# Attention's matmul order drawn by a planner with a charge on each change of kind

## The chip, the cores and the metric

The kernel runs on one core of a Trainium2 chip. The metric is the device time of one execution in microseconds. Three timed runs before the change gave 1975.88, 1974.33 and 1975.59 us, median 1975.59. One more execution was taken with the hardware profiler: its time was 1973.83 us and its span, from the first instruction to the end of the last, 1972.1 us. A difference of about 0.2% (4 us) is what a measurement of this kernel can tell from none.

## The reference

One layer of a hybrid encoder on 1024 positions of width 1024, all in float32. Three token mixers run on the same normalised input; their outputs are gated and summed; a gated feed-forward network follows. Two of the mixers are attention with 8 heads each. Cut to what matters here:

```
def blocked_attention(q, k, v, bias_mask):      # Q_BLOCK = 128, S = 1024
    def one_block(args):
        i, q_blk = args
        s = einsum('bqhd,bkhd->bhqk', q_blk, k) * scale
        p = softmax(bias_mask(i, s), axis=-1)
        return einsum('bhqk,bkhd->bqhd', p, v)

y_a = mla_branch(u_mla, ...) @ w_br_mla          # attention, 8 heads, masked by chunks of 64
y_b = fox_branch(u_fox, ...) @ w_br_fox          # attention, 8 heads, causal, with a decay
y_c = ssm_branch(u_ssm, ...) @ w_br_ssm          # state-space scan in chunks
g = sigmoid(u_gate + b_gate)                     # u_gate = hn @ w_in[..., gate columns]
x = x + (g0 * y_a + g1 * y_b + g2 * y_c) @ w_out
x = x + conv_ffn(rms_norm(x), ...)
```

## The kernel before

Every float32 product is made on TensorE (PE) from a high and a low part of each operand, so most products are three matmuls: high by high, low by high, high by low. The program goes through the layer in stages: projections, the two attentions, the state-space scan, the branch outputs with their gates, the output projection, the feed-forward network. The change lies in the attention stage, from 534.5 to 877 us of the profiled span.

**What the stage does.** There are 16 heads (8 of the first attention, then 8 of the second). Each head has 8 rows of 128 queries; row `i` sees `i + 1` blocks of 128 keys, so its scores are 128 to 1024 columns wide. Two rows make a unit, four units a head. PE does four kinds of work in the stage, named here by the letters of the planner:

- **S**, scores (line 1899, three or two passes a row in pieces of 256 to 512 columns; line 1903 adds the causal mask to the last piece of the second attention's rows). A row's scores stand in a PSUM tile `s`, of which there are two.
- **T**, transposes (line 1966): the normalised probabilities `pm` are turned block by block into a PSUM tile `tp`, up to four blocks to a tile, of which there are two.
- **V**, the product with the values (lines 1978 to 1986): four or five matmuls a tile, added up in PSUM tile `o`.
- **F**, filler (line 1588): the gate columns of the input projection, which nobody in the stage waits for. It comes in steps of six matmuls of 512 columns. What is left of it when the stage ends is done in the state-space scan and shared out there.

Between them stand the other engines. After S, VectorE (DVE) takes the row's maximum (`nmx`, line 1913), ScalarE (ACT) the exponential (`pm`, line 1918), DVE the reciprocal of the sum (`rs`, line 1924), GpSimd (POOL) multiplies by it (line 1926); then T can start. After T, ACT copies the high part (`pth`, line 1970) and DVE subtracts it for the low part (`ptl`, line 1974); then V can start. After the last V of a unit ACT and DVE bring `o` out (lines 1946 and 1950). The scores of a row wait for the exponential of the row two before it, since that frees the tile `s`.

**What sets the order.** PE, ACT, DVE and POOL run in this stage in an order that is fixed when the program is built, and each of them takes its instructions strictly in that order. A planner, class `Sim` from line 1698, draws it: it has a duration and a pace for each task, keeps a clock for each engine, and puts down one instruction after another. For PE it holds one list each for S, T and V and the filler, and `pick_pe` chooses among the heads of the lists that can start earliest; where several can start within 0.02 us, the letters of `ORDER` decide. Filler goes in when nothing else can start within `SLACK`, or when the share of filler done is behind the share of work done (`total` and `lead`).

```
mm_cost(w, n) = n * (w + 32) / 2400        # us for n matmuls of w columns
c = 0.109 * len(offs)                      # us for a tile of transposes
ORDER = "VTS"
sm = Sim(fill, 86, work, 2.0)              # total filler 86 us, lead 2 us
```

Behind the stage, line 2063 shares the filler that is left among the chunks of the scan: `FILL_SSD = [(f_left[0] - 6.0 - 23.0) / 8] * 8 + [12.0, 24.5]`. There `merge` interleaves the pieces of three chunks with filler, for PE alone.

## Time and profile before

| | before |
|---|---|
| median of three runs | 1975.59 us (1974.33 to 1975.88) |
| profiled execution, time | 1973.83 us |
| its span | 1972.1 us |
| granted TensorE clock over the span | 0.999 |
| attention stage, first score to last value product | 534.5 to 876.9 us |
| matmuls in it: S, T, V, F | 544, 576, 704, 444 |
| changes from one kind to another in it | 377 |
| scan behind it, up to the branch products | 877 to 1067 us |

The counts of kinds and changes are those of the program's order; the profile's own rows carry the line numbers by which the kinds are told. A row of the timeline begins with the time at which the instruction started and its duration, both in us. Matmuls overlap: one takes some 0.3 to 0.4 us from start to end, but the next starts 0.06 to 0.23 us after it. So the time that PE needs for a run of matmuls is read from start to start, not from the durations, and PE counts as busy even where it is not at its quickest.

### The profile page before, as it was taken

The page shows a single profiled execution, that of the slowest core. Times are in us where ns is not written, and L with a number is a line of the kernel's source. Part 1 is how long each engine was busy: PE and PEld are TensorE (multiplying, and loading weights), DVE is VectorE, ACT ScalarE, POOL GpSimd, SP SyncE. Part 2 cuts the span into 40 slices and gives each one's busy share as a digit, 9 for nine tenths or more (in the row PEclk, how much of TensorE's full clock was granted, in tenths as well). Part 3 has the DMA queues.
Part 4 walks back from the last instruction along what each step waited for, and adds up shares of the span by engine and source line. Part 5 has one row for each costly group of instructions (what it writes and reads, how often), then busy time and mean ns, then how long its engine had stood idle before and what let it go on. Part 6 is the DMA issues. An engine that isn't in the chain of part 4 may idle for free.

```text
span 1972.1 us, 28446 instructions
## 1 busy us (share of the span) xinstructions
PE 1949.2 (99%) x10053; PEld 1658.6 (84%) x10053; DVE 1401.0 (71%) x2178; ACT 976.9 (50%) x1690; POOL 699.9 (35%) x666
## 2 busy tenths in 40 slices
PE   9999999999999999999999999999999999999999
PEld 8989878888899988887888888888878888888887
DVE  7777769579566676758884575568997877765555
ACT  5555324454566666657783222225544444444432
POOL 5133100166133333213331451102664454423665
PEclk9999999999999999999999999999999999999999
DMA  6166755532757666635646875434222211259575
GB/s 181 53 198 212 202 132 155 187 102 91 227 167 195 177 179 169 170 95 194 214 152 228 291 252 184 139 107 127 94 90 86 76 53 54 86 166 337 185 262 191
DMA packets 281673, 318.46 MB, mean 161 GB/s; under 512 B 19405, under 2 KB 209497, under 8 KB 281530
## 3 DMA queue, kind: packets, MB, share of 16 engines
q1 hardware_dynamic: 281528, 316.64, 51.6%
q8 instruction: 79, 1.29, 0.3%
q14 instruction: 64, 0.52, 0.1%
q10 hardware_dynamic: 2, 0.00, 0.0%
HBM read 223.46 MB, written 93.13 MB: 161 GB/s over the span
## 4 chain that ended last, share of the span: by engine, by line
PE 86%; DVE 5%; issue 3%; ACT 2%; DMA 2%; POOL 1%; SPq 1%; ACTq 0%; DVEq 0%; POOLq 0%
PE dn L2760 10%; PE mm L1588 10%; PE ybr L2328 7%; PE cb L1384 7%; PE ua L2419 6%; PE uc L2419 5%; PE ud L2419 5%; PE wo L2464 4%; PE s L1899 4%; PE fx L798 3%; PE fx L1134 3%; PE tp L1966 3%; PE ub L2419 2%; PE fxv L188 2%; PE py L2172 1%
## 5 line engine op out<-in xcount | busy, mean ns | idle before, releaser
L2760 PE MATMUL dn<-dr,dr 128*128 128x512 f32 x592 | 182.3, 389 | 0.0
L1926 POOL TENSOR_SCALAR pm<-pm,rs 128x128 f32<-128x128 f32 (+7 forms) x128 | 95.3, 747 | 227.1 <-DVE rs L1924 203.6
L1588 PE MATMUL mm<-hnh,wh 128*128 128x512 f32 x320 | 132.6, 414 | 0.3 <-ACT t L1566 0.3
L2760 PEld LDWEIGHTS dn<-dr,dr 128*128 128x128 f32 x592 | 111.2, 188 | 22.9
L1588 PE MATMUL mm<-hnh,wl 128*128 128x512 f32 x320 | 125.7, 393 | 0.0
L1918 ACT ACTIVATE pm<-s,nmx 128x128 f32<-128x128 f32 (+7 forms) x128 | 94.8, 741 | 61.6 <-DVE nmx L1913 52.3
L1588 PE MATMUL mm<-hnl,wh 128*128 128x512 f32 x320 | 125.2, 391 | 0.0
L2760 PE MATMUL dn<-dr 128*128 128x512 f32 x296 | 115.3, 390 | 0.0
L1974 DVE TENSOR_TENSOR ptl<-tp,pth 128x512 fp32r<-128x512 f32 (+1 forms) x160 | 96.8, 632 | 23.7 <-ACT pth L1970 22.4
L135 DVE TENSOR_TENSOR dr<-dr,dr 128x1024 fp32r<-128x1024 f32 x52 | 71.4, 1380 | 51.7 <-ACT dr L134 44.4
L135 DVE TENSOR_TENSOR wl<-S,wh 128x1024 fp32r<-128x1024 f32 x55 | 81.4, 1480 | 35.6 <-ACT wh L134 35.5
L1913 DVE TENSOR_REDUCE nmx<-s 128x1 f32<-128x128 f32 (+7 forms) x128 | 93.4, 748 | 16.0 <-PE s L1899 9.3
L2328 PE MATMUL ybr<-ah,wl 128*128 128x512 f32 x256 | 99.8, 390 | 0.7 <-DVE wl L135 0.7
L2328 PE MATMUL ybr<-al,wh 128*128 128x512 f32 x256 | 99.9, 390 | 0.0
L2328 PE MATMUL ybr<-ah,wh 128*128 128x512 f32 x256 | 99.7, 390 | 0.0
L134 ACT ACTIVATE wh<-wr 128x1024 fp32r<-128x1024 f32 (+1 forms) x47 | 42.4, 902 | 104.6 <-PE ybr L2328 41.2
L1970 ACT ACTIVATE pth<-tp 128x512 fp32r<-128x512 f32 (+1 forms) x160 | 82.7, 553 | 23.1 <-PE tp L1966 21.2
L134 ACT ACTIVATE wh<-S 128x1024 fp32r<-128x1024 f32 x55 | 58.3, 1059 | 67.4 <-PE uc L2419 45.9
L134 ACT ACTIVATE dr<-dr 128x1024 fp32r<-128x1024 f32 x52 | 54.9, 1060 | 71.8 <-PE dn L2760 52.9
L1966 PE MATMUL tp<-ident,pm 128*128 128x128 f32 x576 | 80.9, 273 | 0.2 <-POOL pm L1926 0.2
L135 DVE TENSOR_TENSOR wl<-wr,wh 128x1024 fp32r<-128x1024 f32 (+1 forms) x47 | 54.5, 1159 | 32.9 <-ACT wh L134 32.8
L2637 DVE SCALAR_TENSOR_TENSOR fa<-cg,pc_f,fa 128x1023 f32<-128x1023 f32 (+1 forms) x44 | 74.2, 1688 | 1.4 <-ACT fa L2632 1.4
(665 smaller groups left out, 6219.4 us busy)
## 6 DMA issues: line engine op xcount, KB each, us to landing
dr<-act_d SPq DMA_DIRECT2D x99, 256.0 KB
wr<-in_w_in_dram SPq DMA_DIRECT2D x35, 512.0 KB
raw<-in_w_in_dram SPq DMA_DIRECT2D x27, 512.0 KB
gl<-g_d SPq DMA_DIRECT2D x24, 512.0 KB
wr<-in_ffn_w_up_dram SPq DMA_DIRECT2D x23, 512.0 KB
ws<-in_ffn_w_down_dram SPq DMA_DIRECT2D x22, 512.0 KB
wsum_d<-ws SPq DMA_DIRECT2D x22, 512.0 KB
act_d<-fa SPq DMA_DIRECT2D x22, 512.0 KB
```

Source lines behind the costliest of these rows:

```text
L134: i = A.activation(h, src, AF.Copy) if he is A else he.tensor_copy(h, src)
L135: return i, le.tensor_sub(l, src, f32(h))
L1384: T.matmul(ps, a, b, start=first and i == 0, stop=i == 11, skip_group_check=not first)
L1588: T.matmul(ps, a[:, k, :], b[half][:, k, :], start=(k == 0 and i == 0), stop=(k == NK - 1 and i == 2))
L1913: V.reduce_max(r.nmx[:, 0:1], r.row, axis=AX, negate=True)
L1918: A.activation(r.p[:, 0:cols], r.row, AF.Exp, bias=r.nmx[:, 0:1], accum_out=r.rs[:, 0:1])
L1926: r.norm = Task("G", (d - 0.025, d), lambda: G.tensor_scalar(r.p[:, 0:cols], r.p[:, 0:cols], r.rs[:, 1:2], 0.0, op0=ALU.mult, op1=ALU.add) ...
L1966: T.transpose(x.pt[:, c * P:c * P + P], rows_[qi].p[:, k * P:k * P + P], ident)
L1974: V.tensor_sub(x.tl[:, :off], x.pt[:, :off], f32(x.th[:, :off]))
L2328: T.matmul(pss[half], w_[:, k, :], a_[k][:, hs], start=k == 0 and i == 0, stop=k == nk - 1 and i == 2)
L2419: T.matmul(ps, a, b, start=first and n == 0, stop=n == 11, skip_group_check=not first)
L2760: T.matmul(ps[m], a[:, ts_], b[:, 512:], start=first_ and j == 0 and q == 0, stop=j == NFH - 1 and q == 2, skip_group_check=not first_)
```

## The change

Only the planner's rules change, and so the order in which the same instructions stand. The planner gets a table `SWITCH` with a charge in us for each change from one kind to another (`"TS"`: from transposes to scores), which moves its clock forward, or back where the charge is negative. V must be startable 0.6 us and T 0.4 us longer before they count as ready (`MARGIN`). While it is in a run of S or V it stays there as long as the next of that kind can start (`STICKY`). Once it is in filler, filler counts as behind until it is 2.8 us ahead (`HYST`). Of kinds that are ready together, T now goes first, then V, then S. The total of filler that it aims at in the stage goes from 86 to 80.

```diff
     LATE = 0.09
+    SWITCH = {"TS": 0.155, "TF": 0.117, "TV": 0.122, "SV": 0.088, "SF": 0.075, "FV": 0.037, "VS": 0.035, "VF": 0.051,
+              "VT": -0.049, "ST": -0.039, "FT": -0.075}
+    STICKY, HYST = "SV", 2.8
+    MARGIN = {"V": 0.6, "T": 0.4}
...
-            self.free["P"] = start + c
+            self.free["P"] = start + c + self.enter("F")
...
+        def enter(self, q):
+            x = SWITCH.get(self.kind + q, 0.0)
+            self.kind = q
+            return x
...
-                        c.append((max(x, f), n, st[0], q))
-            t0 = min([e[0] for e in c], default=None)
+                        c[q] = (max(x + MARGIN.get(q, 0.0), f), st[0], q, max(x, f))
+            t0 = min([e[0] for e in c.values()], default=None)
...
-                behind = self.used < self.total * min(1.0, self.worked / self.work) + self.lead
+                due = self.total * min(1.0, self.worked / self.work) + self.lead
+                behind = self.used < due + (HYST if self.kind == "F" else 0.0)
...
-                    e = min((e for e in c if e[0] <= t0 + 0.02), key=lambda e: e[1])
-                    return e[0], e[2], e[3]
+                    if self.kind in STICKY and self.kind in c and c[self.kind][0] <= t0 + 0.03:
+                        return c[self.kind][3], *c[self.kind][1:3]
+                    for q in ORDER:
+                        if q in c and c[q][0] <= t0 + 0.02:
+                            return c[q][3], *c[q][1:3]
...
+                    st += self.enter(q)
                     self.place(x[1], st)
...
-    ORDER = "VTS"
+    ORDER = "TVS"
...
-            sm = Sim(fill, 86, work, 2.0)
+            sm = Sim(fill, 80, work, 2.0)
```

In the stage's order the changes of kind go from 377 to 335, by kind:

| from, to | S-T | S-V | S-F | T-S | T-V | T-F | V-T | V-S | V-F | F-S | F-T | F-V |
|---|---|---|---|---|---|---|---|---|---|---|---|---|
| before | 21 | 42 | 36 | 67 | 14 | 27 | 83 | 14 | 5 | 17 | 4 | 47 |
| now | 45 | 10 | 23 | 18 | 80 | 10 | 27 | 53 | 18 | 6 | 36 | 9 |

Runs of scores become longer (78 runs instead of 99 for the same 544 matmuls), runs of filler fewer (51 for 68), runs of transposes stay 108. Of the filler, 444 matmuls stood in the stage and now 384: 12 go ahead of its first score and 48 behind its last value product. Lines behind the insertions have moved by 4 to 15, so 1899, 1966 and 1978 are 1914, 1981 and 1993 now.

On PE, at a value product in the middle of the first attention, before: the transposes into `tp_6588`, the scores of two rows, and then at once the product that reads the copies of the transposes just made (`pth_6597` is the copy of the tile ahead of `tp_6588`, `pth_6599` that of `tp_6588` itself).

```order
L1966 MATMUL tp_6588<-ident,pm_6450 128x128
L1966 MATMUL tp_6588<-ident,pm_6507 128x128 x2
L1899 MATMUL s_6593<-w0h_6268,w0l_6269 128x512 x3
L1899 MATMUL s_6593<-w0h_6268,w0l_6269 128x384 x3
L1899 MATMUL s_6606<-w0h_6268,w0l_6269 128x512 x3
L1978 MATMUL o<-pth_6597,vv_6274 128x256
...
L1978 MATMUL o<-pth_6599,vv_6274 128x256
```

On PE at the like place now (`pth_7095` is the copy of `tp_7082`):

```order
L1981 MATMUL tp_7082<-ident,pm_6955 128x128
L1981 MATMUL tp_7082<-ident,pm_6969 128x128 x2
L1914 MATMUL s_7089<-w0h_6883,w0l_6884 128x384 x3
L1914 MATMUL s_7089<-w0h_6883,w0l_6884 128x256 x3
L1914 MATMUL s_7104<-w0h_6883,w0l_6884 128x384 x6
L1981 MATMUL tp_7113<-ident,pm_7012 128x128
...
L1981 MATMUL tp_7119<-ident,pm_7077 128x128
...
L1993 MATMUL o<-pth_7069,vv_6578 128x256
...
L1993 MATMUL o<-pth_7095,vv_6578 128x256
```

Both rows' scores now stand in one run, and the next seven transposes have moved in between, so a product stands further behind the transposes that it needs.

On PE, at the scores of a fifth row of the second attention (`s_10053`, 640 columns), before. It takes the place in PSUM of the third row, `s_9994`:

```order
L1899 MATMUL s_9994<-w0h_9803,w0l_9804 128x384 x2
...
L1899 MATMUL s_10000<-w0h_9803,w0l_9804 128x512 x2
...
L1588 MATMUL mm_10011<-hnh_118,wh_9539 128x512
...
L1978 MATMUL o<-pth_9989,vv_9521 128x256
...
L1966 MATMUL tp_10040<-ident,pm_9893 128x128
...
L1966 MATMUL tp_10045<-ident,pm_9905 128x128 x2
L1899 MATMUL s_10053<-w0h_9803,w0l_9804 128x384 x2
```

On PE at the same rows of another head now (`s_9455` takes the place of `s_9408`):

```order
L1914 MATMUL s_9408<-w0h_9206,w0l_9207 128x384 x2
...
L1914 MATMUL s_9415<-w0h_9206,w0l_9207 128x512 x2
...
L1993 MATMUL o<-pth_9395,vv_8875 128x256
...
L1993 MATMUL o<-pth_9401,vv_8875 128x256
...
L1981 MATMUL tp_9435<-ident,pm_9388 128x128 x2
L1914 MATMUL s_9455<-w0h_9206,w0l_9207 128x384 x2
```

Six matmuls of filler, eight of values and seven transposes stood between the fourth row's scores and the fifth's; now nine of values and three transposes do.

On PE at the start of the scan, where `p6`, the six matmuls of line 2146 on `xddh` and `xddl`, wait for their operands; before:

```order
L2117 MATMUL stp_10742<-bc_10622 128x128 x2
L2104 MATMUL stp_10796<-ident,xs_10626 128x128 x4
L1588 MATMUL mm_10722<-hnh_119,wh_10551 128x512
...
L2146 MATMUL pst_10819<-xddh_10754,bTh_10737 128x512
L2146 MATMUL pst_10819<-xddl_10755,bTh_10737 128x512
```

and now:

```order
L2132 MATMUL stp_10682<-bc_10562 128x128 x2
L1588 MATMUL mm_10662<-hnh_119,wh_10475 128x512
...
L2119 MATMUL stp_10750<-ident,xs_10566 128x128 x4
L1588 MATMUL mm_10761<-hnh_118,wh_10625 128x512
...
L2161 MATMUL pst_10777<-xddh_10694,bTh_10677 128x512
L2161 MATMUL pst_10777<-xddl_10695,bTh_10677 128x512
```

A second block of twelve filler matmuls has moved in ahead of the wait. Behind the scan all engines keep their order.

## The prediction

> **What bounds the kernel now.** I read the busy shares and the chain that ended last first, then the stretches by stage, the waits of PE in the stage, and the timeline where PE changes its kind of work.

> ```profile
> PE 1949.2 (99%) x10053; PEld 1658.6 (84%) x10053; DVE 1401.0 (71%) x2178; ACT 976.9 (50%) x1690; POOL 699.9 (35%) x666
> PE 86%; DVE 5%; issue 3%; ACT 2%; DMA 2%; POOL 1%; SPq 1%; ACTq 0%; DVEq 0%; POOLq 0%
> 532.00:877.00 345.00, 342.82 (x2280) 303.95 (x2278) 234.71 (x489) 227.04 (x510) 121.16 (x148) 1.00 0.60 163
> 877.00:900.00 23.00, 20.77 (x96) 16.88 (x97) 10.37 (x11) 14.00 (x34) 5.72 (x2) 0.97 0.94 316
> 900.00:1067.00 167.00, 165.66 (x929) 142.29 (x929) 127.15 (x175) 120.39 (x248) 51.46 (x77) 0.99 0.52 166
> ```

> The stretches give, after their length, the busy time of PE, of its weight loads, of DVE, ACT and POOL, then the granted clock and DMA. PE is busy for 342.8 of the attention stage's 345 us at the full clock, while DVE and ACT have a third of their time free. So the stage lasts as long as PE's own stream of matmuls, and an order can win two things: the time that PE loses in changing from one kind to another, and the short stops in which it waits for ACT, DVE or POOL. How large the first is, the starts tell:

> ```profile
> 540.07 0.29 PE L1978 MATMUL o<-pth,vv 128*128 128x256 f32 x1
> 540.19 0.22 PE L1983 MATMUL o<-pth,vv 128*64 128x128 f32 x1
> 540.25 0.22 PE L1984 MATMUL o<-pth,vv 128*64 128x128 f32 x1
> ...
> 541.43 0.93 PE L1966 MATMUL tp<-ident,pm 128*128 128x128 f32 x7
> 542.12 0.77 PE L1899 MATMUL s<-w0h,w0l 104*128 104x384 f32 x3
> 542.73 0.40 PE L1588 MATMUL mm<-hnh,wh 128*128 128x512 f32 x1
> 542.97 0.39 PE L1588 MATMUL mm<-hnl,wh 128*128 128x512 f32 x1
> 543.19 0.39 PE L1588 MATMUL mm<-hnh,wl 128*128 128x512 f32 x1
> 543.42 0.40 PE L1588 MATMUL mm<-hnh,wh 128*128 128x512 f32 x1
> ```

> From start to start a matmul of 128 columns takes 0.060 us, of 256 0.119, of 512 0.231; by the same reading 384 take 0.174 and a transpose 0.109. Seven transposes and three scores of 384 should then take 7 x 0.109 + 3 x 0.174 = 1.285 us, and took 542.73 - 541.43 = 1.30: that change cost 15 ns. I summed this over all 2,267 intervals from 534.49 to 876.54 us, of which these rows are a part: 327.6 us at those paces, 14.5 us more in fact. Of the 14.5, 3.7 lie in ten intervals that are over 0.25 us too long. These are waits. This is the first, the one right behind it, a third, and the last of the ten:

> ```profile
> 612.75 0.60 PE L1899 MATMUL s<-w0h,w0l 104*128 104x256 f32 x3
> 613.53 0.62 PE L1899 MATMUL s<-w0h,w0l 104*128 104x256 f32 x3 [0.19 <-ACT pm L1918]
> 614.39 0.39 PE L1978 MATMUL o<-pth,vv 128*128 128x256 f32 x1 [0.23 <-DVE o L1950]
> ...
> 800.05 0.27 PE L1966 MATMUL tp<-ident,pm 128*128 128x128 f32 x1
> 800.56 0.55 PE L1966 MATMUL tp<-ident,pm 128*128 128x128 f32 x3 [0.24 <-POOL pm L1926]
> ...
> 862.06 0.35 PE L1978 MATMUL o<-pth,vv 128*128 128x256 f32 x1 [0.22 <-DVE o L1950]
> ```

> Three scores of 256 columns should take 0.36 us; the next started 0.78 us later, so this wait cost 0.42, or 0.35 in its one longest interval. Counted so, two waits before scores come to 0.75 us, seven before value products to 2.56, one before transposes to 0.40. The rest, 10.8 us, is spread over 377 changes and over matmuls a few ns slower than their paces.

> **Switches.** Taking each change as the lateness of the two intervals around it, waits left out, the means are: V-F 41 ns, S-F 37, V-S 32, S-V 26, V-T 25, T-S 15, S-T 14, and the other five between -3 and 4. Times the counts in the table of the change that is 6.5 us before and 5.4 now, so **-1.1 us**. The bounds are 0, if the lateness belongs to the matmuls and not to the change, and -5.3, which is what the table's own charges give (18.9 us before, 13.7 now). I take the value of the rows: 18.9 us of charges is more than all 14.5 us that the stage has to spare, so they must contain waits. The number of transposing runs, which carry the largest charges, stays at 108.

> The row just used has 0.23 us from start to start at 512 columns. [...]

> **Waits before value products.** V needs ACT's copy and DVE's subtraction behind its transposes.

> ```profile
> L1970 ACT ACTIVATE pth<-tp 128x512 fp32r<-128x512 f32 x96 | 54.7, 595 | 11.7 <-PE tp L1966 10.3
> L1970 ACT ACTIVATE pth<-tp 128x384 fp32r<-128x384 f32 x64 | 30.9, 490 | 11.4 <-PE tp L1966 10.9
> L1974 DVE TENSOR_TENSOR ptl<-tp,pth 128x512 fp32r<-128x512 f32 x96 | 63.8, 686 | 15.5 <-ACT pth L1970 15.3
> L1974 DVE TENSOR_TENSOR ptl<-tp,pth 128x384 fp32r<-128x384 f32 x64 | 34.9, 551 | 8.2 <-ACT pth L1970 7.1
> ```

> That is 1.28 us for four blocks and 1.04 for three. I call headroom what PE has to do, at the paces above, between the end of the transposes and the product, less this time. All seven products that waited had a headroom between 0.79 and 1.72 us: it is the queues on ACT and DVE that eat it (the releasers in the rows are the copies of `o`). Below 1.75 us stood 131 of the 160 products before, and 50 stand there now; the pieces of the order show why, with seven transposes and a whole run of scores in between. At the same rate the 2.56 us become 2.56 x 50 / 131 = 0.98: **-1.6 us**, between 0 (the queues decide alone) and -2.56 (none left).

> **Waits before scores.** A row's first scores wait for the maximum and the exponential of the row two before.

> ```profile
> L1913 DVE TENSOR_REDUCE nmx<-s 128x1 f32<-128x384 f32 x16 | 8.8, 548 | 1.1 <-PE s L1899 1.1
> L1913 DVE TENSOR_REDUCE nmx<-s 128x1 f32<-128x1024 f32 x16 | 19.4, 1215 | 0.5 <-PE s L1903 0.3
> L1918 ACT ACTIVATE pm<-s,nmx 128x384 f32<-128x384 f32 x16 | 9.3, 580 | 14.0 <-DVE nmx L1913 12.1 <-POOL pm L1926 1.7
> L1918 ACT ACTIVATE pm<-s,nmx 128x1024 f32<-128x1024 f32 x16 | 17.9, 1117 | 8.3 <-DVE nmx L1913 5.3 <-POOL pm L1926 1.8 <-DVE rs L1924 1.1
> ```

> A row of 384 columns needs 1.13 us, one of 1024 2.33. Before, 5 of 126 rows had less than 0.9 us of headroom over this, and two of the five waited, 0.37 us each. Now 23 rows have less than 0.9, since the runs of scores are longer and filler no longer stands among them. In the piece of the order PE has 0.52 us of the fourth row's scores, 0.90 of values and 0.33 of transposes, together 1.75 us, over the third row's 1.13; before, 3.6. At two in five that makes 23 x 0.4 x 0.37 = 3.4 us: **+2.7 us**, between -0.75 (none waits) and +7.8 (all 23 do). Behind a waiting score the whole of PE stands still, filler too, since PE takes its instructions in order. The one wait of a transpose I leave: it hangs on POOL, whose own work is as before.

> **Filler.** 60 matmuls leave the stage. The next rows are filler where nothing interrupts it.

> ```profile
> 878.69 0.39 PE L1588 MATMUL mm<-hnh,wh 128*128 128x512 f32 x1
> 878.91 0.39 PE L1588 MATMUL mm<-hnl,wh 128*128 128x512 f32 x1
> 879.14 0.39 PE L1588 MATMUL mm<-hnh,wl 128*128 128x512 f32 x1
> ...
> 895.75 0.39 PE L2146 MATMUL pst<-xddh,bTh 128*128 128x512 f32 x1
> 898.17 0.50 PE L2146 MATMUL pst<-xddl,bTh 128*128 128x512 f32 x1 [2.03 <-DVE xddl L135]
> ```

> PE's waits in the scan, by the view of waits (total, times, longest):

> ```profile
> PE pst L2146 <- DVE xddl L135: 2.0, 1, 2.0
> PE stp L2104 <- issue: 1.3, 1, 1.3
> ```

> The stage gets shorter by 60 x 0.231 = 13.9 us, but the matmuls come back at 0.227 us each, 12 ahead of it and 48 in the scan: 13.6. This leaves **-0.2 us**, and a shorter stage is no gain. In the scan they can fill waits. They are 2.0 us for `xddl`, and 1.3 us of another transpose, in one chunk of eight. Twelve more filler matmuls, 2.7 us of PE work, now stand ahead of the first of the two, while the chain that ends in `xddl` begins with transposes that keep their place: **-2.0 us**, between 0 (the chain moves as well) and -3.3 (the other wait goes too). Should the scan's later chunks, where the order of the pieces changes as well, wait 1.3 us in four more places, it would be +5.2 instead.

> **The sum.** -1.1 - 1.6 + 2.7 - 0.2 - 2.0 = -2.2 us on the profiled execution's 1973.83, so 1971.6; the median of the runs lies 1.76 above it, so **1973.4 us**, 0.11% below before.

> **The rivals**, each against the median of 1975.59:

> - *The charges are true.* A change costs what the table says, 5.3 us are won for my 1.1, and all else is as above: 1969.2. For it speaks that the costliest changes, T-S, fall from 67 to 18; against it, that the rows put T-S at 15 ns and that T-V, by the table nearly as dear, rises from 14 to 80. Chance 0.20.
> - *No new waits.* The longer runs of scores wait no more than before (2.7 less): 1970.7. For it, that ACT and DVE have a third of their time free. Against, that they had it when the ten waits happened. Chance 0.07.
> - *The score tiles become the bound.* With two tiles for scores, all 23 rows short of headroom wait 0.37 us, for 8.5 us in place of 0.75; the products wait as before, because the longer runs of scores put two long maxima (1.1 to 1.2 us each) into DVE's queue ahead of the subtractions; the scan's wait is not covered. Then -1.1 + 7.8 - 0.2 = +6.5: 1982.1, slower. It decides from 17 such waits on: 17 x 0.37 - 0.75 - 1.3 (switches and filler) = 4.2 us, just over the 4 that can be told. Against it speaks that three in five such rows did not wait before. Chance 0.20.
> - *The scan takes it back.* The 1.3 us wait comes in four chunks more and the 2.0 us stay: -0.2 + 5.2 = +5.0, 1980.6. Chance 0.08.
> - *The change does not do what it says*: only 42 of 377 changes go, the transposing runs stay as many, and what a switch costs is near nothing. Then the order's effect is within my forecast's own range, and it belongs to its case.

> **How the numbers follow.** The forecast's case, in which gains and new waits about cancel, has a chance of 0.45 and reaches over 1971.6 to 1979.5, which is 0.2% to either side, what a measurement can tell from none. Faster by more: 0.20 + 0.07 = 0.27. Slower by more: 0.20 + 0.08 = 0.28. The range goes from 1966.9, the first rival with no waits left before value products (-1.0 more) and the second wait of the scan covered (-1.3), to 1982.1, the third rival, and leaves out some 0.15.

> **What would show it.** In the profile of after, PE's starts at the paces above should be late by about 5.4 us over the changes: if by less than 3, the charges were true. Waits of value products should come to about 1 us, of scores to some 3 in about nine places, released by the exponential of line 1933. The 2.0 us wait for `xddl` should be gone. The stage from first score to last value product should last 342.4 - 13.9 - 1.1 - 1.6 + 2.7 = 328.5 us. It would prove me wrong if that were over 333 or under 324, or if the scan, with 48 matmuls or 10.9 us more in it, grew by over 13 or under 7.

## The result and the profile after

The changed kernel takes **1979.55 us** (median of 10 runs, 1975.64 to 1982.57) against 1975.17 for the kernel before in 10 runs beside it (1973.01 to 1978.46). The ratio is **1.0019**, 95% interval 1.0011 to 1.0028: slower by 0.2%, where 0.1% faster was forecast. Its profiled execution took 1979.67 us, with a span of 1977.9 us.

The busy shares, the chain that ended last, and the three stretches that answer to those of before (attention, its end, the scan):

```profile
PE 1952.5 (99%) x10053; PEld 1657.5 (84%) x10053; DVE 1408.5 (71%) x2178; ACT 975.1 (49%) x1690; POOL 705.3 (36%) x666
PE 86%; DVE 5%; DMA 3%; issue 3%; ACT 2%; POOL 1%; SPq 1%; ACTq 0%; DVEq 0%; POOLq 0%
538.00:871.00 333.00, 330.59 (x2218) 290.52 (x2217) 232.97 (x487) 222.21 (x505) 121.73 (x148) 1.00 0.59 164
871.00:900.00 29.00, 28.92 (x153) 24.22 (x151) 15.58 (x18) 19.73 (x45) 6.02 (x3) 1.00 0.78 255
900.00:1071.00 171.00, 167.17 (x923) 143.04 (x922) 122.17 (x168) 115.47 (x239) 57.00 (x77) 0.99 0.53 166
```

PE still sets the pace (busy for 330.59 of 333 us). The stretch at the end of attention, where before 2.2 us were idle at a clock of 0.97, is now clean (0.08 us idle, clock 1.00). In the last row 3.8 us are idle, where there were 1.3: what was lost early in the scan is now lost later.

I take the two spans apart by PE's starts: first filler, first score, last value product, first branch product.

| us | before | after | change | of which filler | net |
|---|---|---|---|---|---|
| ahead of the filler | 531.77 | 534.84 | +3.07 | | +3.07 |
| filler ahead of the first score | 2.72 | 5.44 | +2.72 | 12 x 0.227 | 0 |
| attention: first score to last value product | 342.06 | 330.73 | -11.33 | -60 x 0.231 | **+2.5** |
| scan, to the first branch product | 189.57 | 199.88 | +10.31 | 48 x 0.227 | **-0.6** |
| branch products | 175.49 | 176.34 | +0.85 | | +0.85 |
| the rest | 730.52 | 730.71 | +0.2 | | +0.2 |

The first row is not the change's: both kernels do the same there, and over the fourteen profiles of this study the start of this part's last projection (line 1384) lies anywhere from 387.6 to 391.4 us. Before's profile was the earliest of all. In that of after PE stood once for 2.2 us:

```profile
PE tp L1107 <- DVE fqn L1100: 2.9, 2, 2.2
```

That leaves 2.7 us for the rows that the change can touch, inside the interval of the medians (2.2 to 5.5 us). The forecast for them was -2.2.

The waits of PE's weight loads in the attention stage (total, times, longest), first before, then after. Where a product's first matmul has to wait, its weight load, which comes just ahead, waits first, so these rows count more of the waits than PE's own (after has 3.8 us in 10 places here for the two copies of `o`, and 1.0 us in 3 places in PE's):

```profile
PEld o L1978 <- DVE o L1950: 1.5, 3, 0.7
PEld o L1978 <- ACT o L1946: 1.4, 4, 0.4
...
PEld s L1899 <- ACT pm L1918: 0.8, 2, 0.4
```

```profile
PEld o L1993 <- DVE o L1965: 3.1, 9, 0.6
PEld s L1914 <- ACT pm L1933: 2.9, 10, 0.5
...
PEld o L1993 <- ACT o L1961: 0.7, 1, 0.7
```

Score waits went from 0.8 to 2.9 us, as foreseen. Value products did not wait less: 2.9 before, 3.8 now. And the name in front of `o` is the point that the prediction read past: the releasers are the copies of the accumulator (lines 1961 and 1965), not of the transposes.

### The profile page after: what moved, and what is told of

Its sections match the earlier page's. It is cut to its first block, busy times and chain, and to the rows that moved or that the text cites. A ratio compares the mean times of both kernels' runs of the same rounds, so it can differ in the third digit from the quotient of the medians.

```text
span 1977.9 us, 28420 instructions
## 1 busy us (share of the span) xinstructions
PE 1952.5 (99%) x10053; PEld 1657.5 (84%) x10053; DVE 1408.5 (71%) x2178; ACT 975.1 (49%) x1690; POOL 705.3 (36%) x666
## 4 chain that ended last, share of the span: by engine, by line
PE 86%; DVE 5%; DMA 3%; issue 3%; ACT 2%; POOL 1%; SPq 1%; ACTq 0%; DVEq 0%; POOLq 0%
PE mm L1588 11%; PE dn L2775 10%; PE ybr L2343 7%; PE cb L1384 7%; PE ua L2434 6%; PE uc L2434 5%; PE ud L2434 5%; PE wo L2479 4%; PE s L1914 4%; PE fx L798 3%; PE fx L1134 3%; PE tp L1981 3%; PE ub L2434 2%; PE fxv L188 2%; PE py L2187 1%
## 5 line engine op out<-in xcount | busy, mean ns | idle before, releaser
L1588 PE MATMUL mm<-hnh,wh 128*128 128x512 f32 x320 | 131.7, 411 | 0.1
L1588 PE MATMUL mm<-hnh,wl 128*128 128x512 f32 x320 | 125.9, 393 | 0.0
L1588 PE MATMUL mm<-hnl,wh 128*128 128x512 f32 x320 | 125.7, 393 | 0.0
L135 DVE TENSOR_TENSOR dr<-dr,dr 128x1024 fp32r<-128x1024 f32 x52 | 72.3, 1399 | 51.7 <-ACT dr L134 50.0
L135 DVE TENSOR_TENSOR wl<-S,wh 128x1024 fp32r<-128x1024 f32 x55 | 82.6, 1501 | 33.0 <-ACT wh L134 33.0
L135 DVE TENSOR_TENSOR wl<-wr,wh 128x1024 fp32r<-128x1024 f32 (+1 forms) x47 | 56.1, 1194 | 34.1 <-ACT wh L134 34.0
```

The lines of the kernel that those rows point to most:

```text
L135: return i, le.tensor_sub(l, src, f32(h))
L1588: T.matmul(ps, a[:, k, :], b[half][:, k, :], start=(k == 0 and i == 0), stop=(k == NK - 1 and i == 2))
```

## The experiments

Twelve kernels were run, each timed in five rounds against runs of the kernel before on the same chip, from which its ratio is. Names with a_ are the changed kernel with an edit, with b_ the kernel before. All compute the whole layer. The table holds sums over each trace that no single row gives. *Changes* are changes of kind in the stage. *S* and *V* are the waits before scores and value products: what each interval from start to start is longer, by over 40 ns, than the lower quartile of all intervals in the fourteen profiles whose matmul has the same line and size and the same lines before and behind it (this finds shorter waits than the prediction's bound of 250 ns). *Attention* is first score to last value product, less 0.231 us a filler matmul; *rest* takes off all its waits, the few of transposes and filler too. *Scan* runs on to the first branch product, less 0.227 us a filler matmul; *stops* are PE's idle times over 0.3 us in it, *half* the time at the granted clock 0.5; its *rest* takes off the stops and half of that time. The sums are of one execution each. Kernels with the same order in attention (after and a_bc, before and b_bc, and so on) agree in *attention* to 0.1 us; the time of a kernel's single executions differs by up to some 7 us, so a small difference between two scans tells nothing.

| kernel | us | ratio to before | changes | attention | S | V | rest | scan | stops | half | rest |
|---|---|---|---|---|---|---|---|---|---|---|---|
| before | 1975.2 | 1 | 377 | 239.5 | 1.5 | 3.6 | 233.8 | 75.2 | 3.7 | 3.4 | 69.8 |
| after | 1979.6 | 1.0019 | 335 | 242.0 | 4.4 | 3.7 | 232.7 | 74.6 | 3.6 | 3.4 | 69.3 |
| a_ring1 | 1973.2 | 0.9984 | 325 | 235.6 | 1.9 | 0 | 232.7 | 74.1 | 4.1 | 0 | 70.0 |
| b_ring1 | 1978.1 | 1.0007 | 390 | 235.3 | 1.3 | 0.5 | 233.4 | 81.1 | 9.1 | 3.4 | 70.3 |
| a_marginS | 1992.6 | 1.0082 | 338 | 238.8 | 0.4 | 5.1 | 232.7 | 88.5 | 12.5 | 13.6 | 69.2 |
| a_nocharge | 1987.1 | 1.0056 | 366 | 240.5 | 1.7 | 5.3 | 233.0 | 83.9 | 10.2 | 10.2 | 68.6 |
| a_nosticky | 1983.6 | 1.0035 | 394 | 249.0 | 4.3 | 9.7 | 233.2 | 71.8 | 2.4 | 0 | 69.4 |
| a_order | 1982.1 | 1.0029 | 334 | 242.8 | 4.6 | 1.5 | 233.5 | 79.3 | 4.8 | 10.2 | 69.3 |
| b_total80 | 1986.1 | 1.0045 | 376 | 240.0 | 2.2 | 3.8 | 233.9 | 84.2 | 10.1 | 6.8 | 70.7 |
| a_total86 | 1985.7 | 1.0046 | 333 | 243.7 | 5.3 | 3.7 | 232.7 | 79.6 | 7.5 | 3.4 | 70.4 |
| a_bc | 1972.9 | 0.9979 | 335 | 241.9 | 4.4 | 3.7 | 232.7 | 68.5 | 0 | 0 | 68.5 |
| b_bc | 1974.6 | 0.9990 | 377 | 239.6 | 1.5 | 3.6 | 233.9 | 74.6 | 2.2 | 6.8 | 68.9 |
| a_ring1_bc | 1979.4 | 1.0010 | 325 | 235.6 | 1.8 | 0 | 232.8 | 78.0 | 6.5 | 3.4 | 69.8 |
| b_ring1_bc | 1978.0 | 1.0005 | 390 | 235.2 | 1.3 | 0.5 | 233.3 | 78.7 | 7.4 | 3.4 | 69.6 |

The two columns *rest* are the main result. Whatever the order, with 325 or 394 changes, attention takes 232.7 to 233.9 us and the scan 68.5 to 70.7; all else is waits, and in the scan the slow clock behind them. The 95% intervals of the ratios are about 0.0009 to either side where eleven runs stand behind them (a_ring1: 0.9975 to 0.9993; a_bc: 0.9970 to 0.9988) and 0.0013 with five or six.

### The accumulator as one tile: a_ring1, b_ring1

The accumulator `o` is one PSUM tile with two halves, used in turn by the units. The planner takes it for a ring of two (two buffers used in turn), so that a unit's products wait for the copies of the unit two before. In the program they wait for the copies of the unit just before. One digit tells the planner so, in the changed kernel and in the one before:

```diff
-    r_s, r_tp, r_o, r_pm, r_th = Rel(2), Rel(2), Rel(2), Rel(PM), Rel(TH)
+    r_s, r_tp, r_o, r_pm, r_th = Rel(2), Rel(2), Rel(1), Rel(PM), Rel(TH)
```

> The changed kernel with one number of the planner different: it takes the accumulator o as a ring of one tile (r_o = Rel(1)), so a unit's first value product is planned behind the copy of the unit just before, not of the unit two before. Theory 'one accumulator': o is one PSUM tile for both halves, so the program waits for the previous unit's copy whatever the planner thinks; told so, the planner puts other work there. Then waits over 40 ns before value products fall from 3.7 us (12) to under 1 us, and first score to last value product, less 0.231 us for each filler matmul, gets 2 to 4 us shorter. Rival 'queues': the waits come from long maxima ahead of the subtractions on DVE; then they stay above 2.5 us. Time between 1974 and 1979 by the first, 1978 to 1982 by the second.

> The kernel before with the same one number (r_o = Rel(1)) and nothing of the change. 'One accumulator': waits over 40 ns before value products fall from 3.6 us (15) to under 1 us, with the changes of kind as many as before (390), and the time falls by 1 to 4 us below before. 'Queues': the waits stay above 2.5 us and the time within 1 us of before.

First the wait in the changed kernel, in the timeline of PE, and DVE's and ACT's rows beside it:

```profile
804.57 0.33 PE L2001 MATMUL o<-ptl,vv 128*128 128x256 f32 x1
804.76 0.86 PE L1914 MATMUL s<-qk,qk 128*128 128x384 f32 x4
805.46 0.23 PE L1918 MATMUL s<-mfox,identb 128*128 128x128 bf16 x1
805.53 0.61 PE L1981 MATMUL tp<-ident,pm 128*128 128x128 f32 x4
806.50 0.39 PE L1993 MATMUL o<-pth,vv 128*128 128x256 f32 x1 [0.37 <-DVE o L1965]
```

```profile
804.86 0.67 DVE L1928 TENSOR_REDUCE nmx<-s 128x1 f32<-128x512 f32 x1
805.45 0.68 DVE L1989 TENSOR_TENSOR ptl<-tp,pth 128x512 fp32r<-128x512 f32 x1
806.04 0.41 DVE L1965 TENSOR_TENSOR o<-o,o 64x256 f32<-64x256 f32 x1
```

```profile
803.55 0.60 ACT L1985 ACTIVATE pth<-tp 128x512 fp32r<-128x512 f32 x1 [0.83 <-PE tp L1981]
...
804.60 0.60 ACT L1985 ACTIVATE pth<-tp 128x512 fp32r<-128x512 f32 x1
805.22 0.38 ACT L1961 ACTIVATE o<-o 64x256 f32<-64x256 f32 x1
```

One unit ends on PE at 804.9. ACT's copy of it starts at 805.22, DVE's at 806.04, and at 806.50, right behind its end, the next unit's product starts. That product's own `pth` is the copy that began at 803.55; it was there at 804.15, its `ptl` at 804.87. The headroom behind its transposes, which the prediction counted, does not come into it. The copies of `o` stand in the queues of ACT and DVE like everything else: DVE's came behind a maximum and the subtraction for a later product.

Who waited for `o` in the stage (total, times), in the changed kernel, then in a_ring1:

```profile
  PEld o L1993: 3.8, 10
...
  PE o L1993: 1.0, 3
```

```profile
  DVE o L1965: 17.2, 26
  ACT o L1961: 13.1, 19
  ACT pth L1985: 2.7, 2
  POOL pm L1941: 1.4, 2
```

PE's rows are gone; 3.7 us become 0, and in the kernel before 3.6 become 0.5. The theory of one accumulator holds, and its rival, that long maxima ahead of the subtractions make the products wait, falls: the waits went with a digit that concerns `o` alone. With the plan right on this, the change's attention (235.6) is level with the old order's (235.3). In time only a_ring1 gains; what b_ring1 wins in attention, 4.2 us, its scan gives back with 5.9, so that the 1 to 4 us expected of it did not come.

### What makes scores wait: a_marginS, a_nocharge, a_nosticky, a_order

Four single edits of the changed kernel: scores must be startable 0.4 us longer; no charges; no staying in a run; the old order of letters.

```diff
-    MARGIN = {"V": 0.6, "T": 0.4}
+    MARGIN = {"V": 0.6, "T": 0.4, "S": 0.4}
```

```diff
-    SWITCH = {"TS": 0.155, "TF": 0.117, "TV": 0.122, "SV": 0.088, "SF": 0.075, "FV": 0.037, "VS": 0.035, "VF": 0.051,
-              "VT": -0.049, "ST": -0.039, "FT": -0.075}
+    SWITCH = {}
```

```diff
-    STICKY, HYST = "SV", 2.8
+    STICKY, HYST = "", 2.8
```

```diff
-    ORDER = "TVS"
+    ORDER = "VTS"
```

> The changed kernel with a margin for scores too (0.4 us longer startable before they count as ready). Theory 'score tiles': the waits before scores (4.4 us over 40 ns in 33 places) come from rows planned too close behind the exponential two rows back; then they fall below 1.5 us, waits before value products stay at 3 to 4, and the stage less its filler gets 2 to 4 us shorter. Rival: they come from ACT's queue and move along with the order; then they stay above 3 us.

> The changed kernel with the table of charges empty and all else of the change kept (margins, sticky runs, transposes first): 366 changes of kind in place of 335. Theory 'a change of kind is free': the parts of the stage that are no wait stay as they are (10.0 us over the paces, within 0.7), and only the waits differ: before scores they fall below 3 us, since runs of scores are shorter. Rival 'the charges are real': those parts rise by 2 us or more, as 31 more changes at 0.05 to 0.15 us each would.

> The changed kernel, with the rule that keeps PE in a run of scores or values taken out. The program has 110 runs of scores for 78 of the changed kernel, 394 changes of kind for 335, the same 384 filler matmuls in the stage. If the score waits come from the longer runs of scores: they fall from 4.4 us to about 1.5 (as before the change), the value waits stay at 3.7, and the stage is 3 us shorter than the changed kernel's 330.7, about 328. If they come from transposes going first among kinds that are ready together (which this kernel keeps): they stay at 4.4 and the stage lasts 330 to 331. If a change of kind costs what the planner's table charges, the 59 more changes cost some 2 us more; if it costs nothing, the part of the lateness that goes with the place of a matmul stays at 6.2 to 6.6 us. Of the scan I only expect that its time less filler lies anywhere from 74 to 84 us.

> The changed kernel, with values before transposes before scores among kinds that are ready together, as before the change. The program has 334 changes of kind, 69 runs of scores, longer still than the changed kernel's 78, and 432 filler matmuls in the stage; 504 stand behind it, as many as before the change. If the score waits come from the longer runs of scores: they are 4 us or more here. If they come from transposes going first: they fall to about 1.5 us. With 504 filler matmuls behind the stage the scan should last what it lasted before the change, 189.6 us, and have the wait for xddl of 2.0 us, if the scan's waits hang on the number of filler matmuls in it; if they hang on which of them falls where, it can be anything from 188 to 200.

The margin takes the score waits away (4.4 to 0.4), and the stage's own time falls by 3.2 us: they were real, and the order could avoid them. Value waits rose to 5.1, over the 3 to 4 expected, and the kernel is slower all the same, by its scan. Without charges the score waits fall to 1.7, but not for the reason expected: the runs of scores are 78 as before that edit.

The last two answer which rule brought them. In a_nosticky the runs of scores are short again (110, for 78), and the waits are still 4.3; with transposes no longer first, in a_order, 4.6. Weight loads in the stage, a_nosticky and then a_order:

```profile
PEld o L1993 <- DVE o L1965: 6.5, 15, 0.7
PEld s L1914 <- ACT pm L1933: 3.6, 9, 0.9
PEld o L1993 <- ACT o L1961: 3.5, 7, 0.7
```

```profile
PEld s L1914 <- ACT pm L1933: 4.3, 13, 0.5
```

So neither the longer runs of scores nor transposes going first is needed for the waits. The attention stage of a_nosticky misses its forecast by 10 us because value waits rose to 9.7, which no theory had foreseen; its scan, at 71.8, lay outside the expected 74 to 84 too. In a_order the scan lasted 193.7 us, not the 189.6 of before, with as many filler matmuls, and the wait for `xddl` is not in it: so the waits there hang on which filler falls where.

What all kernels with 4 us and more share is the charges together with the accumulator taken for two. Either taken away leaves 1.7 or 1.9: no charges (a_nocharge), or charges with one accumulator (a_ring1). They share the margins for V and T and `HYST` as well, and no run took these out, so the cause stays open in part. One may argue that the charges make the planner's PE slower than the real one (13.7 us of charges, of which the starts below show next to nothing), so that scores arrive earlier than planned. No run shows that step, and a_ring1 says that it is not enough by itself.

**A change of kind as such costs next to nothing.** With 366 and 394 changes for 335, *rest* moves by 0.3 and 0.5 us, some 10 ns a change. Priced by the planner's table the order of a_nosticky costs 16.6 us against 13.7, so 2.9 us more; that of a_nocharge only 0.2 more (13.9), so that the 2 us expected of it by "the charges are real" were wrongly worked out and it tests little. Over all fourteen profiles the two intervals around a change from transposes to scores, the dearest in the table at 155 ns, are 5 ns late in the median, from transposes to filler 3, to values 2. What the prediction took for the price of a change goes with certain matmuls. One is a tile's last product: the lateness of a tile's last value matmul (line 1986), waits over 250 ns left in, median and count by what follows, is

| ns late | then S | then T | then F | then V |
|---|---|---|---|---|
| before, diagonal tile | 52 (8) | 54 (38) | 50 (4) | 48 (13) |
| before, full tile | -1 (6) | 2 (45) | -5 (1) | 1 (44) |
| after, diagonal tile | 54 (30) | 54 (10) | 51 (9) | 50 (14) |
| after, full tile | 1 (23) | 1 (17) | -2 (8) | 1 (48) |

A diagonal tile has three matmuls of half size ahead of its last. It is 50 ns late whether the next matmul is another kind or the same, and there are 64 such tiles in any order. The rows at 804.57 and 804.76 above are one: 0.19 us for 0.12.

The other is the mask product of the second attention (line 1903, now 1918), and here what follows does count. Over the fourteen profiles it and the next matmul are 85, 84 and 82 ns late in the median before scores, filler and values (666 places), taking the mask at 40 ns (its median from start to start ahead of these in before and after; 67 to 69 ahead of a transpose), and 34 before a transpose (230 places), so 50 ns less. Of the 64 masks 4 stood ahead of a transpose before the change and 24 do after it: 20 x 50 ns are 1.0 of the 1.1 us by which *rest* fell.

### The total of filler: b_total80, a_total86

The total alone, in the kernel before and undone in the changed one:

```diff
-            sm = Sim(fill, 86, work, 2.0)
+            sm = Sim(fill, 80, work, 2.0)
```

> The kernel before with the planner's filler aim at 80 in place of 86: no charge, no margin; 24 filler matmuls move from the attention stage to the scan. Theory 'the scan pays for nothing': the 2.0 us wait for xddl is covered by the filler that moves in, but transposes of a later chunk wait longer, and the scan grows by its 24 x 0.227 = 5.4 us within 1.5; the time stays within 2 us of before. Rival 'filler fills': the scan grows by under 3 us and the time falls by 2 to 4.

> The changed kernel, with the planner's filler total at 86 as before the change. The program has 408 filler matmuls in the stage and 528 behind it (384 and 552 in the changed kernel), 333 changes of kind. If the total of 80 is what costs time: this is 3 us or more below the changed kernel. If the attention waits do not depend on it: score waits 4 us and value waits 3.5 us remain, the stage less 0.231 us a filler matmul stays at 242 (so 336 us long), and the difference in time is the scan's alone, in either direction.

Before with 80 is 0.45% slower, after with 86 too (0.46%), 6 us above after. The number is not the cause, then. Attention waits hardly differ from those of the same rules with the other total (3.6 to 3.8 us of value products in all four kernels; of scores 2.2 for 1.5 and 5.3 for 4.4). The time goes in the scan: 84.2 and 79.6 for 75.2 and 74.6. The sizes were missed in both expectations, since neither had the scan move by so much on its own.

### Where the scan stops: a_bc, b_bc, a_ring1_bc, b_ring1_bc

PE's waits in the scan of the changed kernel, and the place of the longest, in its timeline:

```profile
PE stp L2119 <- issue: 3.6, 2, 2.2
PE stp L2119 <- PE stp L2222: 0.2, 1, 0.2
```

```profile
1007.82 0.39 PE L2132 MATMUL stp<-bc 128*128 128x128 f32 x2
...
1012.53 0.61 PE L2222 MATMUL stp<-ident,y 128*128 128x128 f32 x4
1015.35 0.84 PE L2119 MATMUL stp<-ident,xs 128*128 128x128 f32 x4 [2.22 <-issue]
1015.84 0.78 PE L1588 MATMUL mm<-hnh,wh 128*128 128x512 f32 x1
1016.42 0.63 PE L1588 MATMUL mm<-hnl,wh 128*128 128x512 f32 x1
1016.84 0.63 PE L1588 MATMUL mm<-hnh,wl 128*128 128x512 f32 x1
```

The `xddl` wait of before is gone, and the transposes of x, which waited once for 1.34 us, now wait twice, 1.37 and 2.22 us. "issue" names no releaser; DVE's rows do, with POOL's beside them:

```profile
1008.51 2.27 DVE L135 TENSOR_TENSOR xddl<-xdd,xddh 128x1024 fp32r<-128x1024 f32 x1 [0.58 <-ACT xddh L134]
...
1011.64 1.21 DVE L135 TENSOR_TENSOR hsl<-hst,hsh 128x1024 fp32r<-128x1024 f32 x1
...
1013.38 1.21 DVE L1560 TENSOR_TENSOR wl<-wr,wh 128x1024 fp32r<-128x1024 f32 x1
1014.51 0.41 DVE L135 TENSOR_TENSOR bTl<-stp,bTh 128x256 fp32r<-128x256 f32 x1
1014.85 0.40 DVE L2135 TENSOR_TENSOR cbm<-stp,tri 128x256 f32<-128x256 f32 x1
```

```profile
1004.45 2.94 POOL L2142 TENSOR_TENSOR xdd<-xT,dend 128x1024 f32<-128x1024 f32 x1 [3.49 <-ACT xT L2120]
1007.35 2.35 POOL L2144 TENSOR_TENSOR y<-xT,Db 128x1024 f32<-128x1024 f32 x1
```

The `stp` tiles are a ring of two. The tile that B and C filled (line 2132) is read last by `cbm`, which stands behind a row of other operations of DVE, from `xddl` on, and ends at 1015.25; 0.1 us later the transposes of x start, which take its place. One of the row, line 1560, is the filler's own split of weights. The edit puts the tile of B and C into the other ring:

```diff
-            pt = psp.tile([P, 4, P], F32, name=uid("stp"), tag="tp", bufs=2)
+            pt = psp.tile([P, 4, P], F32, name=uid("stb"), tag="st", bufs=2)
```

> The changed kernel with one tile of the scan moved: the four products and transposes of B and C (lines 2130 and 2132) get a PSUM tile of the ring that the state products use, not of the ring of the x transposes (line 2119), so that these no longer wait for DVE to read them. Theory 'the scan's ring': the three waits of line 2119 (1.37, 0.24 and 2.22 us) and the half clock behind the longest go; last value product to first branch product, less 0.227 us for each filler matmul in it, falls from 74.6 us to 70 or less, and the time by 3 to 6 us below the changed kernel. Rival 'DVE is late for everyone': the wait moves to the next user of the ring (lines 2130, 2161), and that figure stays above 73.

> The kernel before with the same tile moved and nothing of the change. 'The scan's ring': its wait of 1.34 us on line 2104 goes, the wait of 2.03 us for xddl and the half clock behind it stay, the scan less its filler falls from 75.2 to about 74 us, the time by about 1 us. Against the changed kernel with the tile moved it then shows the change without this ring: the attention stage less its filler 2.5 us shorter here, the scan 3 to 4 us longer, so the two times within 2 us. 'DVE is late for everyone': no gain here, and the changed kernel stays 3 to 5 us above.

> Both single edits together on the changed kernel: the planner's one accumulator and the scan's tile. If the two causes are separate, the attention stage keeps the 328.2 us of the first edit, the scan less its filler falls from 74.1 to 71 or less, and the time is 3 to 5 us below that edit alone (1968 to 1971). If the scan's waits hang on where the filler falls and not on the ring, it stays within 1 us of the first edit alone.

> The kernel before, with both edits: the planner takes the accumulator o as one tile, and the transposes of B and C stand in the other ring. The attention stage should be that of the first edit alone: 332.3 us with 420 filler matmuls, value waits about 0.5 us, 4 us less lateness than before. If the ring of the B and C tiles was what gave back that gain in the first edit alone (scan less filler 81.1 us): the scan less filler is 75 or below and the time about 1971. If the scan's waits hang on where filler falls, whatever the ring: the scan less filler is 78 to 82, and the time no better than 1975.

In a_bc the view of PE's waits is empty from 865 to 1075 us, and at the same place nothing stands still:

```profile
1008.91 0.60 PE L2222 MATMUL stp<-ident,y 128*128 128x128 f32 x4
1009.36 0.60 PE L2119 MATMUL stp<-ident,xs 128*128 128x128 f32 x4
1009.71 0.48 PE L1588 MATMUL mm<-hnh,wh 128*128 128x512 f32 x1
```

The scan falls by 6.1 us and the kernel to **1972.92 us**, the lowest median, though not told apart from that of a_ring1. b_bc loses the wait of line 2104 and keeps that for `xddl`, as expected. With this ring the changed order is ahead of the old one, 1972.92 to 1974.60, though the two intervals overlap.

The two good edits do not add up, and neither theory of a_ring1_bc foresaw it: the attention stays won (235.6), but the scan stops, now for the other ring:

```profile
PE stb L2130 <- DVE yo L2198: 5.2, 2, 4.2
PE pst L2161 <- DVE xddl L135: 1.3, 1, 1.3
```

b_ring1_bc stops there too, 2.5 us, and 2.4 us for `xddl`, so its second theory was right. Read together, the ring decides which tile PE waits for, and the place of the filler whether it waits: in b_total80 its total alone moved the scan by 9 us.

## Why the prediction was wrong

- **What bounds the kernel**: right. PE is busy for 330.6 of 333 us, and *rest* is nearly constant.
- **Switches, -1.1**: the size came, in part by luck. *Rest* fell by 1.1 us, 233.8 to 232.7, but nearly all of that is the mask product, which has a transpose behind it 20 times more (above). The prediction's means held this (S-F 37 and S-V 26 ns against S-T 14), but as the price of a change, beside prices for leaving V and T that are none. Counted in the prediction's way, the changes are late by 8.5 us and not by 5.4, because many of the new score waits are under its bound of 250 ns. The first rival (true charges) is out: the table has 5.3 us between the two orders, and 2.9 between a_nosticky and after, where *rest* has 1.1 and 0.5.
- **Waits before value products, -1.6: the failed step.** The prediction measured the distance from a product to its transposes, said that "the queues on ACT and DVE" eat it, and put the releaser, the copies of `o`, in brackets. That releaser was the cause. The headroom rose from 1.24 to 2.11 us in the median, as foreseen, and the waits stayed, 3.6 to 3.7 us, until the plan knew of the one accumulator. By the prediction's own bound of 250 ns they went from 2.56 to 2.05 us, so -0.5.
- **Waits before scores, +2.7**: +2.9 with all waits over 40 ns, which is luck in the number. It is spread over 33 places of 0.13 us on average, not nine of 0.37; by the prediction's own bound there are five, and they add 0.8 us. The length of the runs of scores is not why (a_nosticky).
- **Filler, -0.2**: taken over as priced, -13.86 and +13.62; no run tests the two paces apart from the rest.
- **Scan, -2.0: mis-sized, -0.6 came.** The `xddl` wait (2.0 us) and the 3.4 us at half clock behind it are gone, with twelve more filler matmuls ahead of it. The x transposes, which the prediction let wait four times more only as a mishap of +5.2, took most of it back: 3.6 us for 1.3, and 3.4 us at half clock of their own. That is a part of the fourth rival, inside the forecast's own case.
- **Branch products**, costed at nothing: +0.85, with a stop of 1.1 us for a weight split in place of 0.7.

The two missed steps, 1.7 and 1.4 us, and this one come to 4.0 of the 4.9 us between -2.2 and +2.7; the rest is in terms of 0.5 us and less, short waits of filler the largest. The stage lasted 330.7 us for the 328.5 forecast, and the scan grew by 10.3 for 10.9, inside the bounds set for both. So the tests written down would not have caught it; the releaser in the waits' rows did.

## What to carry to other kernels

When a wait's row names a releaser, count the distance to that releaser, and see in the program which tile's turn the semaphore stands for; here two halves of one tile counted as one. If a planner draws an order, correct what it believes about rings before tuning its prices: one digit won 4.2 and 6.4 us of attention, and without the table of charges attention was 1.5 us shorter. Judge an order by all stages that its leftovers reach: how much filler was left and where it fell changed the scan by up to 14 us (74.6 to 88.5), more than any order won in attention.

## What the hardware showed beside that

**Half clock behind long stops.** Behind PE's stop of 2.22 us the matmuls of 512 columns start 0.43 us apart (1016.42 to 1016.84) in place of 0.23. The stretches around that place, with the granted clock as the third number from the end:

```profile
971.00:1015.00 44.00, 42.13 (x240) 36.23 (x239) 36.19 (x49) 33.63 (x74) 16.56 (x20) 1.00 0.52 168
1015.00:1020.00 5.00, 4.65 (x16) 3.85 (x17) 4.99 (x8) 2.61 (x5) 0.54 (x1) 0.66 0.92 257
```

The half clock lasts 3.41 us (here from 1015.63 to 1019.04), or twice that (a_order has 10.2 us of it behind two stops). By the starts just given (0.43 for 0.23 us) it costs about half of that time where PE has work, which is an estimate. In the scans of the fourteen profiles 16 of 21 stops of 1.8 to 4.2 us had it behind them; of the shorter ones none but a pair of 1.57 and 1.49 us, 0.5 us apart. a_marginS is the worst, with four such stretches behind five stops. These are its waits, and the 3.41 us ahead of the first stretch, that stretch and the second:

```profile
PE stp L2119 <- issue: 10.3, 5, 2.3
```

```profile
933.20:936.61 3.41, 1.47 (x13) 1.20 (x11) 3.41 (x8) 3.13 (x9) 0.00 (x0) 1.00 0.14 42
936.61:940.02 3.41, 3.36 (x10) 2.90 (x11) 3.41 (x5) 1.12 (x2) 0.00 (x0) 0.50 0.73 186
960.50:963.91 3.41, 3.41 (x11) 2.83 (x11) 3.41 (x6) 1.77 (x3) 0.00 (x0) 0.50 0.71 247
```

**DVE's subtraction beside POOL.** The subtraction for `xddl` began at 1008.51 and took 2.27 us; the one for `hsl`, as large, took 1.21. POOL's line 2144 ran until 1009.70, and from there to the end at 1010.78 are 1.08 us. The fourteen profiles have 98 such subtractions: the 36 that began while POOL was at that line end 1.08 or 1.09 us behind its end, the other 62 take 1.20 to 1.23. Since DVE's row runs on without a gap from there to `cbm`, some 1 us of its delay may come from this (2.27 less 1.21, an estimate); no run changed POOL's work by itself.
